# One decoder layer: output weights kept split for the second half, five banks for the gates, one PSUM pool

## The chip, the cores and the metric

The kernel runs on one core of a Trainium2 chip. The metric is the device time of one execution in microseconds. Before the change three runs took 2130.45, 2126.56 and 2125.76 us, with a median of 2126.56.

## The reference

One layer of a causal decoder, 1024 positions, 1024 features, all in float32. Two token mixers work side by side: a sparse attention (an indexer picks up to 256 keys for each query) and a stick-breaking attention. Their outputs are projected by `w_o_a` and `w_o_b`, gated, added, and projected by `w_out` into the residual stream. A gated feed-forward network stands before and behind.

```python
x = x + 1/2 * swiglu(rms_norm(x, g_ffn1), w1_gate, w1_up, w1_down)
proj = rms_norm(x, g_mix) @ w_in        # c_q, k_a, v_a, k_idx, w_idx, q_b, k_b, v_b, gate_a, gate_b
y_a = dsa_attention(...)                # (1024, 512), 8 heads of 64
y_b = stick_breaking_attention(...)     # (1024, 512)
merged = sigmoid(gate_a) * (y_a @ w_o_a) + sigmoid(gate_b) * (y_b @ w_o_b)
x = x + merged @ w_out
x = x + 1/2 * swiglu(rms_norm(x, g_ffn2), w2_gate, w2_up, w2_down)
```

## The kernel before

**Arithmetic.** TensorE multiplies in a rounded 32-bit format. To keep float32 accuracy every operand is held as a high part (rounded) and a low part (what the rounding left), and a product is three matmuls, high by high, high by low and low by high: `mm3`, lines 312 to 314. To split a weight, ACT copies it into the high part and POOL subtracts (`split`, lines 299 and 301; in the attention stage lines 1124 and 1126); `halve` does this for activations (lines 386 and 387). Weights that are needed twice can be kept in DRAM as parts: `split_of` names them, and line 1115 loads such parts without any splitting. In names, a last "h" or "l" is the part, and "r" is the raw weight.

**Stages.** The feed-forward network before runs to about 660 us, then come the projections of the mixers. From about 740 to 1368 us runs the stage "attend", in which both attentions, the gates' projections and the output projections of the first half of the positions are woven into one list. Then the second half of the positions is merged ("psm", to 1391 us: y of the sparse attention by `w_o_a`, times the gate on line 2262, plus the other mixer's part). Then `project` multiplies by `w_out`, for the first half to 1436 us and for the second to 1484 us ("psout"; the sum goes into x on line 2294), and the second feed-forward network runs to the end. Between the two projections' ends, x is normalised for that network: squares on ACT (line 428), mean and root (`rsqrt`, lines 288 and 290, the root on POOL), the product "by" on DVE (line 434), and transposes of "by" on TensorE ("pst", line 448).

**Order.** Each engine takes its own list strictly in order. Outside "attend" a scheduler writes the lists. Inside, the class `Weave` does: each piece of work is a generator that yields the engine of its next step and what it needs, and `Weave` gives every step a time from a cost estimate (`cost`) and always takes the one that can start first. The lists come from these estimates alone. All loads from DRAM stand in SP's list, most stores in POOL's (`put_low`).

**Buffers.** A `Ring` hands out a fixed number of buffers, and who wants one waits until it is given back. Accumulators in PSUM come from rings of banks: three "ubank", two "vbank", one "wbank", two "fbank". The gates' projections ("psf", in `fproj`) and the values' ("psuv", in `proj_uv`) use "fbank". A gate's bank is emptied by ACT's sigmoid into an "ev" buffer (`gate_out`, lines 1230 to 1235), of which there are three, and which comes free when POOL's store of it into `gd` has landed; "psuv" needs two of the three (`uv_out`, lines 1241 to 1248). The output weights "oa0", "oa2", "oa4", "oa6" (columns of `w_o_a` for the first half) and behind them "woa0" and "woa2" (the same weights again, for the second half) go through a ring of two raw buffers and one of four part buffers, that is two weights at a time.

**The attention's end.** A head's output leaves "pso" through ACT and DVE ("yt", lines 1891 and 1893) and is split into "y" (ACT line 2085, DVE line 2087). "psL" are the logits (lines 2037 and 2038), which DVE takes out of PSUM with their maximum "mx" (line 1991). "psoa" is the product of y by "oa". "y10" to "y13" are pairs of heads of the second half, y13 the last.

## Time and profile before

| | |
|---|---|
| three runs | 2125.76 to 2130.45 us, median 2126.56 |
| the profiled execution | 2126.26 us, span 2124.5 us |
| TensorE (PE) busy | 2100.6 us, 99% of the span, 10196 instructions |
| DVE, ACT, POOL busy | 1521.6, 1063.6 and 913.5 us (72, 50 and 43%) |
| DMA | 387.79 MB, 183 GB/s in the mean |
| 600 to 700 us | PE busy 97.85 of 100 us |
| 1040 to 1130 us | PE busy 86.99 of 90 us |
| 1300 to 1345 us | PE busy 42.44 of 45 us |
| 1460 to 1520 us | PE busy 59.39 of 60 us |

Times in the profile are microseconds from the start of the span. PE is TensorE, PEld its loading of weights, DVE VectorE, ACT ScalarE, POOL GpSimd, SP the engine whose queue issues the loads. A row of the timeline has the start, the duration, the engine, the line, the operation and "out<-in"; "x4" means that four instructions are drawn together; the bracket tells how long the engine had been idle and what released it. Ends of matmuls are modelled, so the distance between starts says more than their durations.

### The profile page before, as it was taken

How to read it: one execution, taken by the hardware profiler on the slowest of the kernel's cores; microseconds unless marked ns; L12 is line 12 of the kernel's file. 1: busy time of each engine (PE TensorE's matmuls, PEld its weight loads, DVE VectorE, ACT ScalarE, POOL GpSimd, SP SyncE). 2: the span in 40 equal slices, each digit the busy share in tenths (PEclk: the TensorE clock that was granted, in tenths of full speed). 3: DMA queues.
4: the chain of work that ended last, by engine and by line, in shares of the span. 5: the costliest groups of instructions: out<-in, count | busy, mean ns of one | idle time of the engine just before them, and what ended most of it. 6: DMA issues, size and time to landing. Idle time of an engine off the chain costs nothing.

```text
span 2124.5 us, 29820 instructions
## 1 busy us (share of the span) xinstructions
PE 2100.6 (99%) x10196; PEld 1762.4 (83%) x10196; DVE 1521.6 (72%) x2477; ACT 1063.6 (50%) x1998; POOL 913.5 (43%) x717
## 2 busy tenths in 40 slices
PE   8999999999999999999999999999999999999999
PEld 7888888888889988888887888778888888888887
DVE  7866767678875599788886588754755556488675
ACT  6343343334455356888886577535432322324443
POOL 6654555522345234322123342255665545542233
PEclk9999999999999999999999999999999999999999
DMA  5577877497685253686647755574143333259655
GB/s 150 160 245 219 251 203 237 151 328 249 212 231 167 76 159 105 224 217 165 171 157 231 258 165 169 190 257 151 50 129 100 104 95 129 95 185 330 222 175 188
DMA packets 298104, 387.79 MB, mean 183 GB/s; under 512 B 40144, under 2 KB 186224, under 8 KB 297952
## 3 DMA queue, kind: packets, MB, share of 16 engines
q1 hardware_dynamic: 285088, 343.90, 52.2%
q0 software_dynamic: 12864, 41.99, 5.5%
q8 instruction: 80, 1.31, 0.3%
q14 instruction: 72, 0.59, 0.1%
HBM read 264.67 MB, written 121.15 MB: 182 GB/s over the span
## 4 chain that ended last, share of the span: by engine, by line
PE 88%; issue 4%; DVE 3%; DMA 3%; POOL 1%; ACT 1%; SPq 0%; POOLq 0%; DVEq 0%; ACTq 0%
PE p L774 6%; PE p L775 6%; PE p L773 6%; PE pd L535 4%; PE pd L534 3%; PE pd L536 3%; PE pc L534 3%; PE pa L535 3%; PE pa L534 3%; PE pa L536 3%; PE pc L535 3%; PE pc L536 3%; PE psf L312 3%; PE psf L313 3%; PE psf L314 3%
## 5 line engine op out<-in xcount | busy, mean ns | idle before, releaser
L1374 ACT ACTIVATE junka<-u,cand,sig 128x1024 bf16<-128x1024 f32 (+3 forms) x124 | 134.5, 1085 | 5.0 <-DVE cand L1366 3.6
L1820 DVE TENSOR_TENSOR_SCAN left<-left,hidden 128x640 f32<-128x640 f32 (+3 forms) x64 | 88.9, 1409 | 2.0 <-ACT left L1814 1.8
L897 ACT ACTIVATE swh<-swr 128x512 fp32r<-128x512 f32 x48 | 30.2, 629 | 115.5 <-issue 52.5
L898 DVE TENSOR_TENSOR swr<-swr,swh 128x512 f32<-128x512 f32 x48 | 43.6, 908 | 37.8 <-ACT swh L897 37.6
L677 ACT ACTIVATE b0u<-b0u 128x512 f32<-128x512 f32 x20 | 12.6, 632 | 99.8 <-DVE b0u L557 84.4
L1874 DVE SCALAR_TENSOR_TENSOR pt<-pstT,pt 128x512 fp32r<-128x512 f32 (+1 forms) x96 | 51.4, 547 | 14.4 <-ACT pt L1871 13.8
L1871 ACT ACTIVATE pt<-pstT 128x512 fp32r<-128x512 f32 (+1 forms) x96 | 46.6, 495 | 16.6 <-PE pstT L1946 15.1
L1726 ACT ACTIVATE relu<-psdot 128x512 f32<-128x512 f32 (+1 forms) x80 | 40.7, 522 | 26.5 <-DVE u L1733 17.4
L1235 POOL DMA_DIRECT2D gd<-evg x32 | 18.0, 564 | 80.4 <-ACT evg L1230 59.4
L774 PE MATMUL p<-aT,aS 128*128 128x512 f32 x132 | 51.5, 390 | 1.0 <-DVE aT L387 1.0
L774 PE MATMUL p<-bT,bS 128*128 128x512 f32 x132 | 51.3, 389 | 0.0
L1733 DVE SCALAR_TENSOR_TENSOR u<-relu,WI,u 128x512 f32<-128x512 f32 (+1 forms) x70 | 49.2, 718 | 2.7 <-ACT relu L1726 1.7
L775 PE MATMUL p<-aT,aS 128*128 128x512 f32 x132 | 50.7, 389 | 0.0
L775 PE MATMUL p<-bT,bS 128*128 128x512 f32 x132 | 50.7, 389 | 0.0
L2000 ACT ACTIVATE e<-e,mx 128x768 f32<-128x768 f32 (+7 forms) x54 | 40.9, 759 | 13.3 <-DVE mx L1991 13.1
L773 PE MATMUL p<-bT,bS 128*128 128x512 f32 x132 | 47.0, 389 | 0.0
L1946 PE MATMUL pstT<-ident,left 128*128 128x128 f32 x288 | 45.8, 272 | 0.0
L773 PE MATMUL p<-aT,aS 128*128 128x512 f32 x132 | 44.9, 389 | 0.0
L1814 ACT ACTIVATE left<-psz 128x512 f32<-128x512 f32 (+2 forms) x96 | 43.4, 507 | 1.7 <-PE psz L1839 1.6
L1946 PEld LDWEIGHTS pstT<-ident,left 128*128 128x128 f32 x288 | 35.7, 140 | 8.2
L1370 DVE TENSOR_SCALAR_CACHE_REDUCE junkv<-u,cand 128x512 uint8<-128x512 f32 (+1 forms) x62 | 41.7, 673 | 0.8
L386 ACT ACTIVATE bT<-bt 128x512 fp32r<-128x512 f32 x44 | 26.2, 624 | 30.9 <-PE p L775 26.7
(3065 smaller groups left out, 8135.4 us busy)
## 6 DMA issues: line engine op xcount, KB each, us to landing
aw<-in_w_down_dram SPq DMA_DIRECT2D x33, 512.0 KB, 4.9
bw<-in_w_down_dram SPq DMA_DIRECT2D x33, 512.0 KB, 5.0
swr<-in_w_in_dram SPq DMA_DIRECT2D x48, 256.0 KB, 5.6
a0r<-in_w_gate_dram SPq DMA_DIRECT2D x22, 512.0 KB, 7.5
a1r<-in_w_up_dram SPq DMA_DIRECT2D x22, 512.0 KB, 7.2
b0r<-in_w_gate_dram SPq DMA_DIRECT2D x22, 512.0 KB, 4.1
b1r<-in_w_up_dram SPq DMA_DIRECT2D x22, 512.0 KB, 3.9
x<-in_x_dram SPq DMA_DIRECT2D x16, 512.0 KB, 6.2
```

What stands on the lines that cost most here:

```text
L312: nc.tensor.matmul(ps, ah, bh, start=first, stop=False)
L313: nc.tensor.matmul(ps, ah, bl, start=False, stop=False)
L314: nc.tensor.matmul(ps, al, bh, start=False, stop=last)
L534: nc.tensor.matmul(ps, a[:, c], b[k][:, HI], start=start and k == 0, stop=False, skip_group_check=True)
L535: nc.tensor.matmul(ps, a[:, c], b[k][:, LO], start=False, stop=False, skip_group_check=True)
L536: ins = nc.tensor.matmul(ps, a[:, l], b[k][:, HI], start=False, stop=k == 3, skip_group_check=True)
L773: nc.tensor.matmul(ps[q][m], S[:, h], T[:, HI], start=p == 0, stop=False)
L774: nc.tensor.matmul(ps[q][m], S[:, h], T[:, LO], start=False, stop=False)
L775: nc.tensor.matmul(ps[q][m], S[:, l], T[:, HI], start=False, stop=p == last)
L1374: nc.scalar.activation(junks[1][:, 0:(i + 1) * P], score[i], AF.Sign, scale=sig[:, b:b + 1], bias=cand.bitcast(F32)[:, b:b + 1], accum_out ...
L1820: nc.vector.tensor_tensor_scan(back, back, ones, 1.0, op0=ALU.mult, op1=ALU.max)
L1946: nc.tensor.transpose(tp[:, q * P:(q + 1) * P], A[n + q][:, j * P:(j + 1) * P], ident)
```

## The change

Six things change together; TensorE does the same matmuls.

1. *Parts kept.* While "oa" is used in "attend", a new stream `weights_out` stores its parts into DRAM as "woa0" to "woa6", and the merge of the second half loads them. In `project` the first half stores its parts of `w_out`, and the second half loads them. 12 raw loads with their 12 copies on ACT and 12 subtractions on POOL go, 24 stores on POOL's queue and 24 loads of parts on SP's come.
2. *Banks for the gates.* Between the marks "sparse" and "warm", gates and "psuv" may use "ubank" as well as "fbank" (`filling`), whichever is free first.
3. *Scattered durations.* `Weave` multiplies each estimated duration, except TensorE's, by a random factor between 0.97 and 1.03 (fixed seed).
4. *One PSUM pool.* One pool serves all stages, with the banks by name, where each stage had one of its own.
5. *The merge's order.* In "psm" the first four blocks take y10 to y12 first and y13 later, in an order that is written out.
6. *Steps.* POOL's subtraction of the "oa" weights goes in four steps of 256 columns.

The diff, cut to its core (in the changed kernel lines lie 4 to 59 lines further down):

```diff
@@ class Weave
+        self.luck = random.Random(67)
...
                 cost, late = self.cost(i, eng, outs, ins)
+                cost *= self.luck.uniform(1 - 0.03, 1 + 0.03) if eng != PE else 1.0
@@ def banks
+            turn[letter] += 1
+            return (first if letter == "a" else psum).tile([P, 512], F32, tag=f"{letter}{1 - turn[letter] % 2}", name=name, bufs=1)
@@ split_of: the parts that are kept in DRAM
+                for nm in (*columns, *(f"woa{d}" for d in range(0, ND, 2)), *(f"wout{n}{j}" for n in range(2) for j in range(0, ND, 2)))}
@@ PSUM pools
-    fpsum = ctxf.enter_context(tc.tile_pool(name="psf", bufs=1, space=PSUM))
+    fpsum, psum = (ctxf.enter_context(tc.tile_pool(name=f"ps{name}", bufs=1, space=PSUM)) for name in "fx")
...
-        ubank, vbank, wbank = (ring_of(tiles_of(psum), tag, bufs, (P, 512)) for tag, bufs in (("u", 3), ("v", 2), ("w", 1)))
-        fbank = ring_of(tiles_of(fpsum), "a", 2, (P, 512))
+        ubank, vbank, wbank = (bank_ring(psum, *tags) for tags in (("b0", "b1", "c0"), ("c1", "d0"), ("d1",)))
+        fbank = bank_ring(fpsum, "a0", "a1")
@@ def weights
-                nc.gpsimd.tensor_tensor(wl[:, 0:m], raw[:, 0:m], f32(wh[:, 0:m]), op=ALU.subtract)
+                step = 256 if nm[:2] == "oa" else m
+                for c in range(0, m, step):
+                    yield POOL, raw, wh
+                    c = slice(c, c + step)
+                    nc.gpsimd.tensor_tensor(wl[:, c], raw[:, c], f32(wh[:, c]), op=ALU.subtract)
@@ gates
+        def filling():
+
+            return [fbank, ubank] if "sparse" in weave.marks and "warm" not in weave.marks else [fbank]
+
+        def first_of(rings):
+            return min(rings, key=lambda r: weave.when((r,), PE))
...
-            ps = fbank("psf")
+            ps = first_of(rings or [fbank])("psf")
...
-            ps, vt, (uvh, uvl) = fbank("psuv"), VT[t], UV
+            ps, vt, (uvh, uvl) = first_of(rings)("psuv"), VT[t], UV
@@ attend's outputs
+        def weights_out(nm, *parts):
+            for to, w in zip(split_of[nm], parts):
+                weave.held[w.tensor.name] += 1
+                yield POOL, w
+                put_low(to, f32(w))
+                give(w)
...
+                if nm == "oa":
+                    spawn(weights_out(f"woa{d}", *W.parts))
@@ the merge of the second half
-                wh, wl = first.pop(0) if first else wcols(w_o_a, d * P, 2 * P, 0, 4, f"woa{d}")
...
-                    for k in range(4):
-                        c = slice((2 * k + e) * P, (2 * k + e + 1) * P)
-                        mm3(ps, wh[:, c], wl[:, c], Y[1][k][:, HI], Y[1][k][:, LO], k == 0, k == 3)
+            def output_weights(d):
+                if first:
+                    return first.pop(0)
+                W = [rpool.tile([P, 1024], F32R, tag="r", name=f"woa{d}{part}", bufs=NR) for part in "hl"]
+                for w, part in zip(W, split_of[f"woa{d}"]):
+                    nc.sync.dma_start(f32(w), part)
+                return W
...
+            with tc.manual_schedule(engines={nc.tensor.engine}):
+                at = {(d, e): begun(d, e, W[d], range(3)) for d, e in pairs[:4]}
+                for d, e in pairs[:4]:
+                    ended_(d, e, onward(d, e, W[d], (3,), at[d, e]))
+                for d, e in pairs[4:]:
+                    ended_(d, e, begun(d, e, W[d], range(4)))
@@ def project
-                        Ws[j] = wcols(w_out, n * 512, 512, j, 2, f"wout{half}{n}{j}", rawt=raw, wt=op)
+                        kept = split_of[f"wout{n}{j}"]
+                        if half:
+                            Ws[j] = [op(f"wout1{n}{j}{x}") for x in "hl"]
+                            for w, d in zip(Ws[j], kept):
+                                nc.sync.dma_start(f32(w), d)
+                        else:
+                            Ws[j] = wcols(w_out, n * 512, 512, j, 2, f"wout0{n}{j}", rawt=raw, wt=op)
+                            for w, d in zip(Ws[j], kept):
+                                nc.gpsimd.dma_start(d, f32(w))
```

Three places in TensorE's list, and one in SP's. First TensorE in the stage "attend", at the gate blocks wg1 and wg2, before:

```order
L1926 MATMUL psy_11206<-pt_11197,vv_10720 128x256 [waits Activation_49]
L1928 MATMUL psy_11206<-pt_11197,vv_10720 128x256 [waits DVE_49]
L1926 MATMUL psy_11206<-pt_11215,vv_10720 128x128 [waits Activation_49]
L1928 MATMUL psy_11206<-pt_11215,vv_10720 128x128 [waits DVE_49]
L312 MATMUL psf_11253<-mhi0_5617,wg1h_10898 128x512 [waits Activation_49]
L313 MATMUL psf_11253<-mlo0_5625,wg1h_10898 128x512
L314 MATMUL psf_11253<-mhi0_5617,wg1l_10899 128x512
```

The first matmul into the bank psf_11253 waits for ACT. So do, 24 rows on, the next two banks' first rows, for DVE and for ACT:

```order
L312 MATMUL psuv_11297<-uvh_8838,vt_11241 128x512 [waits DMAHW3_49,DVE_49]
L313 MATMUL psuv_11297<-uvl_8839,vt_11241 128x512
L314 MATMUL psuv_11297<-uvh_8838,vt_11241 128x512 [waits DMAHW4_49]
L312 MATMUL psf_11330<-mhi0_5617,wg2h_11125 128x512 [waits DMAHW7_49,Activation_49]
L313 MATMUL psf_11330<-mlo0_5625,wg2h_11125 128x512
```

After the change the same matmuls read:

```order
L316 MATMUL psf_11265<-mhi0_5641,wg1h_10955 128x512
L317 MATMUL psf_11265<-mlo0_5649,wg1h_10955 128x512
L318 MATMUL psf_11265<-mhi0_5641,wg1l_10956 128x512
L316 MATMUL psf_11265<-mhi1_5642,wg1h_10955 128x512
L317 MATMUL psf_11265<-mlo1_5650,wg1h_10955 128x512
```

There is no wait here, and at the next two banks:

```order
L316 MATMUL psuv_11324<-uvh_8889,vt_11176 128x512 [waits DMAHW1_49]
L317 MATMUL psuv_11324<-uvl_8890,vt_11176 128x512
L318 MATMUL psuv_11324<-uvh_8889,vt_11176 128x512 [waits DMAHW2_49]
L316 MATMUL psf_11335<-mhi0_5641,wg2h_11160 128x512 [waits DMAHW7_49]
L317 MATMUL psf_11335<-mlo0_5649,wg2h_11160 128x512
L318 MATMUL psf_11335<-mhi0_5641,wg2l_11161 128x512 [waits DMAHW0_49]
```

The matmuls are the same ones. The waits for ACT and DVE at the first matmul of a bank are gone; those for loads are left.

Second, TensorE at the end of "attend" and the start of the merge, before ("pso" is the last head, "psm" the merge on the parts of woa0):

```order
L2102 MATMUL pso_13955<-pt_14001,vh_13709 128x128 x2
L2102 MATMUL pso_13955<-morep0_12157,vh_13709 128x256 [waits Activation_49]
L2102 MATMUL pso_13955<-morep0_12157,vh_13709 128x256 [waits DVE_49]
L312 MATMUL psm_14049<-y10_12153,woa0h_13869 128x512 [waits DVE_49]
L313 MATMUL psm_14049<-y10_12153,woa0h_13869 128x512
L314 MATMUL psm_14049<-y10_12153,woa0l_13870 128x512
```

and after, from the last matmuls on "oa6" to the first on "woa2":

```order
L316 MATMUL psoa_14035<-y03_11361,oa6h_13850 128x512
L317 MATMUL psoa_14035<-y03_11361,oa6h_13850 128x512
L318 MATMUL psoa_14035<-y03_11361,oa6l_13851 128x512
L316 MATMUL psm_14104<-y12_12175,woa0h_13948 128x512
L317 MATMUL psm_14104<-y12_12175,woa0h_13948 128x512
L318 MATMUL psm_14104<-y12_12175,woa0l_13949 128x512
L316 MATMUL psm_14117<-y10_12173,woa2h_14058 128x512 [waits DMAHW4_49,PE_49]
L317 MATMUL psm_14117<-y10_12173,woa2h_14058 128x512
L318 MATMUL psm_14117<-y10_12173,woa2l_14059 128x512 [waits DMAHW5_49]
```

Before, the first "psm" on woa0 followed the last "pso" and waited for DVE. Now the last "pso" stands ahead of the 12 rows of this "psoa", 21 rows of "psm" on y10 to y12 follow them, and the first matmul on "woa2h" waits for a load, three rows behind the last on "oa6l".

SP's list after, around that load ("woa2hd" is the stored part in DRAM, "gd" the gates):

```order
L2290 DMA gate_14101<-gd_108 128x512 [waits DMAHW3_49]
L1124 DMA woa2h_14058<-woa2hd_174 128x1024 [waits DMAHW4_49,DMASW6_49,PE_49]
L1124 DMA woa2l_14059<-woa2ld_175 128x1024 [waits DMAHW5_49,DMASW7_49,PE_49]
L2291 DMA gate_14101<-obd_117 128x512 [waits DMAHW6_49]
L2290 DMA gate_14114<-gd_108 128x512 [waits DMAHW7_49]
```

The load of woa2h waits for TensorE (PE), since its buffer held oa6h.

Third, TensorE where the first half's projection by `w_out` ends and the second half's begins, before ("psg" is a transpose of the gains):

```order
L313 MATMUL psout_14373<-wout016l_14500,m07_14223 128x512
L314 MATMUL psout_14373<-wout016h_14498,m07_14223 128x512
L414 MATMUL psg_14551<-ident_71,bg_14549 128x8 [waits DMAHW2_49,DVE_49]
L312 MATMUL psout_14595<-wout100h_14601,m10_14412 128x512 [waits DMAHW4_49,DMAHW5_49,DMAHW3_49,DMAHW6_49,DMAHW1_49,DMAHW7_49,DMAHW0_49,Activation_49]
L313 MATMUL psout_14595<-wout100l_14603,m10_14412 128x512 [waits Pool_49]
L314 MATMUL psout_14595<-wout100h_14601,m10_14412 128x512
```

and after:

```order
L318 MATMUL psout_14412<-wout016h_14543,m07_14253 128x512
L453 MATMUL pst_14782<-ident_71,by00_14602 128x128 [waits DVE_49,Activation_49]
L453 MATMUL pst_14789<-ident_71,by00_14602 128x128
L453 MATMUL pst_14796<-ident_71,by00_14602 128x128
L453 MATMUL pst_14782<-ident_71,by01_14603 128x128 [waits DVE_49,Activation_49]
L453 MATMUL pst_14789<-ident_71,by01_14603 128x128
L453 MATMUL pst_14796<-ident_71,by01_14603 128x128
L453 MATMUL pst_14782<-ident_71,by02_14604 128x128 [waits DVE_49,Activation_49]
```

Rows of the same kind follow for by02 and by03, and then:

```order
L453 MATMUL pst_14796<-ident_71,by03_14605 128x128
L453 MATMUL pst_14803<-ident_71,by00_14602 128x128 [waits DVE_49]
L453 MATMUL pst_14803<-ident_71,by01_14603 128x128
L453 MATMUL pst_14803<-ident_71,by02_14604 128x128
L453 MATMUL pst_14803<-ident_71,by03_14605 128x128
L316 MATMUL psout_14642<-wout100h_14646,m10_14455 128x512 [waits DMAHW7_49,DMAHW2_49,DMAHW1_49]
```

Before, the second projection followed at once. Now the 16 transposes of by00 to by03 stand between the two, each first one waiting for DVE and ACT, and the first matmul on "wout100h" is behind the last of them.

More of the change, by code (lines that the diff above doesn't have):

```diff
@@ L330, in in_turn, with banks @@
         return tile_
-    def banks(psum, first=None):
-        at = [0]
+    def banks(psum, first):
+        at, turn = [0], defaultdict(int)
         def bank(name, letter=None):
@@ L1062, in trunk @@
     fp = tc.tile_pool(name="sf", bufs=1)
-    psm = tc.tile_pool(name="psm", bufs=1, space=PSUM)
-    with fp as fpool, psm as psum, tc.manual_schedule(
+    with fp as fpool, tc.manual_schedule(
             engines={nc.tensor.engine, nc.vector.engine, nc.scalar.engine, nc.gpsimd.engine}):
@@ L1307, in fillers @@
                 for half in range(2):
-                    yield PE, fbank, late(3)
-                    ps, cols = yield from fproj(s.parts, half, lambda: late(3))
+                    rings = filling()
+                    yield PE, rings, late(3)
+                    ps, cols = yield from fproj(s.parts, half, lambda: late(3), rings)
                     outs.append(spawn(gate_out(ps, g, cols)))
@@ L1313, in fillers @@
                     t = len(UVS)
-                    if gates.index(g) >= UV_FROM and t < NT and weave.when(("uv", f"vt{t}", fbank), PE) <= weave.free[PE]:
+                    if gates.index(g) >= UV_FROM and t < NT and weave.when(("uv", f"vt{t}", filling()), PE) <= weave.free[PE]:
                         yield from proj_uv(t)
@@ L2241, in trunk @@
         heads_.close()
[L2244 removed]
+    with ctxf, tc.tile_pool(name="ring2", bufs=1) as rpool:
         op, raw = ring(rpool)
@@ new lines, in begun, with onward @@
+            def begun(d, e, W, ks):
+                r = slice((d + e) * P, (d + e + 1) * P)
+                g = ht("gate", F32)
+                nc.sync.dma_start(g[:, 0:512], gd[r, 512:1024])
+                nc.sync.dma_start(g[:, 512:1024], obd[r, 512:1024])
+                return onward(d, e, W, ks, (bank("psm", "bcda"[(d + e) % 4]), g))
+            def onward(d, e, W, ks, at):
+                for k in ks:
+                    c = slice((2 * k + e) * P, (2 * k + e + 1) * P)
+                    mm3(at[0], W[0][:, c], W[1][:, c], Y[1][k][:, HI], Y[1][k][:, LO], k == 0, k == 3)
+                return at
```

35 lines of the change are left out of this document (17 added, 18 removed).

## The prediction

> **What bounds the kernel now.** I read the busy times and the table of stretches first, then the waits of TensorE, then its timeline around each wait, and last the engines that end these waits. From the page and the table (columns: stretch in us, its length, busy us and instructions of PE, PEld, DVE, ACT, POOL, granted clock, DMA share, GB/s):
>
> ```profile
> PE 2100.6 (99%) x10196; PEld 1762.4 (83%) x10196; DVE 1521.6 (72%) x2477; ACT 1063.6 (50%) x1998; POOL 913.5 (43%) x717
> ...
> 1300.00:1345.00 45.00, 42.44 (x224) 34.45 (x223) 42.52 (x88) 31.87 (x57) 12.31 (x10) 1.00 0.58 182
> 1345.00:1400.00 55.00, 52.18 (x249) 42.56 (x249) 42.63 (x60) 25.36 (x39) 22.59 (x13) 0.97 0.55 192
> 1400.00:1460.00 60.00, 60.00 (x272) 49.58 (x271) 24.45 (x36) 23.31 (x32) 31.44 (x17) 1.00 0.75 261
> ```
>
> TensorE is busy 2100.6 of 2124.5 us, so the whole idle time that any edit can win is 23.9 us, while its instructions are as many after the change as before. Between 1400 and 1460 us it never stops: 272 matmuls in 60 us, one every 0.22 us, and this is why the splittings of weights that ACT and POOL no longer do win nothing there. A change shows only where TensorE waits, or where it stands in a new place behind something late. The waits of TensorE (line, releaser; total us, times, longest):
>
> ```profile
> PE psL L2037 <- DVE mx L1991: 2.4, 2, 2.2
> ...
> PE psdot L1755 <- ACT relu L1726: 1.7, 4, 0.6
> PE psf L312 <- ACT evg L1230: 1.5, 2, 1.2
> PE psf L312 <- DVE evl L1243: 1.5, 1, 1.5
> PE psm L312 <- DVE yt L1893: 1.4, 1, 1.4
> ...
> PE psout L313 <- POOL wout000l L301: 1.3, 1, 1.3
> ```
>
> The change comes to all of these but "psdot". I take them in order of time, and then two places where the new order makes TensorE wait.
>
> **Gates, more banks.** TensorE around the three waits of the gate projections (start, us, instruction; idle before it in brackets), then ACT's evictions and the landing of the stores from "evg":
>
> ```profile
> 1113.82 0.28 PE L1928 MATMUL psy<-pt,vv 128*128 128x128 f32 x1
> 1115.26 0.50 PE L312 MATMUL psf<-mhi,wg1h 128*128 128x512 f32 x1 [1.17 <-ACT evg L1230]
> ...
> 1121.29 0.39 PE L314 MATMUL psuv<-uvh,vt 128*128 128x512 f32 x1
> 1122.04 0.50 PE L312 MATMUL psf<-mhi,wg2h 128*128 128x512 f32 x1 [0.37 <-ACT evg L1230]
> ...
> 1127.39 0.39 PE L314 MATMUL psf<-mhi,wg2l 128*128 128x512 f32 x1
> 1129.25 0.50 PE L312 MATMUL psf<-mhi,wg2h 128*128 128x512 f32 x1 [1.47 <-DVE evl L1243]
> ```
>
> ```profile
> 1114.64 0.57 ACT L1230 ACTIVATE evg<-psf 128x512 f32<-128x512 f32 x1
> 1121.42 0.57 ACT L1230 ACTIVATE evg<-psf 128x512 f32<-128x512 f32 x1
> 1129.20 0.60 ACT L1230 ACTIVATE evg<-psf 128x512 f32<-128x512 f32 x1 [1.05 <-DMA gd<-evg]
> ```
>
> ```profile
> DMA to landing us min/median/max: 2.3/4.6/8.9
> ```
>
> From start to start, less 0.1 us for a matmul of 128 columns and 0.23 us for one of 512, the three cost 1.34, 0.52 and 1.63 us, 3.5 in all. The banks are held because their eviction waits for one of the three "ev" buffers, and these come free when a store has landed (median 4.6 us). In the new order none of these three rows waits for ACT or DVE, since five banks serve instead of two. The buffers are not more, though, so part may come back some banks later: bounds −3.5 and 0. ACT's evictions come 6.8 and 7.8 us apart, and one gate half with its "psuv" is 27 matmuls, 6.1 us: the lag is 0.7 to 1.7 us a round, and three banks more hold several rounds. I take −3.0.
>
> **Subtractions of w_o_a in four steps.** TensorE, DVE and POOL at the longest wait of all:
>
> ```profile
> 1340.15 0.39 PE L314 MATMUL psoa<-y,oa4l 128*128 128x512 f32 x1
> 1342.75 0.45 PE L2037 MATMUL psL<-kkh,qs 128*128 128x384 f32 x1 [2.21 <-DVE mx L1991]
> ```
>
> ```profile
> 1339.20 2.90 DVE L2087 TENSOR_TENSOR y<-yt,y 128x512 fp32r<-128x512 f32 x1
> ...
> 1342.62 0.68 DVE L2191 TENSOR_TENSOR o<-psoa,both 128x512 f32<-128x512 f32 x1
> ```
>
> ```profile
> 1339.18 2.38 POOL L1126 TENSOR_TENSOR oa6l<-oa6r,oa6h 128x1024 fp32r<-128x1024 f32 x1 [5.83 <-ACT oa6h L1124]
> ```
>
> DVE's subtraction of 128x512 takes 2.90 us where the like of it takes 0.68: it began 0.02 us after POOL's and ended after it. The 2.2 us that it was late are TensorE's 2.21. A step of 256 columns is an estimated 0.6 us (a quarter of 2.38), so DVE loses 0 to 0.6 us instead of 2.2. DVE is busy 42.5 of these 45 us, and gets a few divisions from ACT; at 0.7 us each (as the 0.68 of the row), one or two of them may land here. I take −1.9, bounds −2.2 and −0.5.
>
> **The last head.** TensorE where the second half's merge begins:
>
> ```profile
> 1367.07 0.85 PE L2102 MATMUL pso<-morep,vh 128*128 128x256 f32 x2
> 1369.32 0.53 PE L312 MATMUL psm<-y,woa0h 128*128 128x512 f32 x1 [1.41 <-DVE yt L1893]
> 1369.66 0.62 PE L313 MATMUL psm<-y,woa0h 128*128 128x512 f32 x1
> 1370.08 0.63 PE L314 MATMUL psm<-y,woa0l 128*128 128x512 f32 x1
> ...
> 1373.06 0.40 PE L312 MATMUL psm<-y,woa0h 128*128 128x512 f32 x1
> ```
>
> The wait is 1.41 us, and behind it the matmuls start 0.43 us apart until 1373.06 (the granted clock of the stretch is 0.97): eight steps in 3.40 us that take 1.8 at 0.23, so 1.6 more. With 0.45 us lost inside the pair at 1367.07 (0.85 where two of 256 columns need 0.4 at most), the place costs 3.5. In the new order 12 matmuls of "psoa" and 21 of "psm" stand between the last "pso" and the first that needs y13. They cover 33 x 0.23 = 7.6 us, and evicting the head took 2.25 us (1367.07 to 1369.32). All 3.5 go; bounds −3.5 and −1.9 (a slow stretch left to what comes).
>
> **Stored w_o_a, loaded late.** This is the first new wait. "woa2h" and "woa2l" get the buffers of "oa6h" and "oa6l". Their loads therefore stand in SP's queue until TensorE has finished the last "psoa", and in the new order only three matmuls (0.7 us) lie between that and the first one on "woa2h". In before, ACT and POOL split woa2 at 1359 us, so nothing waited. Of how long such a load of 512 KB takes the trace has the loads of the stored halves of other weights (L1115):
>
> ```profile
> L1115 SPq DMA_DIRECT2D wqk5200h<-wqk5200hd x1: 320/320/320, 679.5 to 679.5; - x1
> ...
> DMA to landing us min/median/max: 3.2/4.8/10.1
> ```
>
> At the least it costs 3.2 − 0.7 = 2.5 us, at the median 4.8 − 0.7 = 4.1; I take 3.8, nearer to the median, as queues are 0.55 busy here. Behind "woa2h" waits all the rest of TensorE's list; SP holds gate loads behind it that are needed later. The Trainium skill, "DMA: Bandwidth & Descriptors", section on the anatomy of one DMA, has about 2.0 us fixed and the bytes at 436 GB/s; by it, an estimate, 512 KB take 3.2 us. That is the least that the trace has, its median is 1.6 us over it, and the sum would be 1.3 us lower. The loads of woa0, woa4 and woa6 have some 28 matmuls or more ahead of their first use, 6.3 us and more, and I cost them nothing; if woa0's took the longest landing, it would be late by 10.1 − 6.3 = 3.8.
>
> **The border of the two projections.** The second new wait. TensorE and then DVE in before:
>
> ```profile
> 1436.07 0.39 PE L314 MATMUL psout<-wout016h,m 128*128 128x512 f32 x1
> 1436.54 0.50 PE L312 MATMUL psout<-wout100h,m 128*128 128x512 f32 x1
> ...
> 1458.48 3.65 PE L448 MATMUL pst<-ident,by 128*128 128x128 f32 x32
> ```
>
> ```profile
> 1436.49 0.69 DVE L2294 TENSOR_TENSOR x<-x,psout 128x512 f32<-128x512 f32 x1 [0.67 <-PE psout L314]
> ...
> 1437.67 0.15 DVE L288 TENSOR_SCALAR ms<-ss 128x1 f32<-128x1 f32 x1 [0.42 <-ACT by L428]
> ...
> 1441.67 0.14 DVE L288 TENSOR_SCALAR ms<-ss 128x1 f32<-128x1 f32 x1
> 1442.49 0.88 DVE L434 TENSOR_SCALAR by<-x,rs 128x512 f32<-128x512 f32 x2 [0.68 <-POOL rs L290]
> 1443.29 0.14 DVE L288 TENSOR_SCALAR ms<-ss 128x1 f32<-128x1 f32 x1
> ```
>
> The transposes of "by" run at 1458.48, 22 us after the last matmul of the first projection, long after "by" is ready. In the new order 16 of them stand directly behind that matmul and ahead of the first "wout100". They need the whole chain: the last addition into x starts 0.42 us after that matmul and takes 0.69; then per row tile a mean on DVE, a root on POOL and two products on DVE, 1.62 us (1441.67 to 1443.29), one tile after the other, as DVE's list has them. From 0.42 + 0.69 = 1.1 us, three tiles (4.9) and the fourth's first product (0.15 + 0.68 + 0.44 = 1.3) make 7.3; the second product and a copy of the gains (0.6) stand ahead of the last four transposes (0.11 each): TensorE goes on at about 8.4. In before it went on at 0.47. The 16 transposes are done meanwhile, 16 x 0.114 = 1.8. So 8.4 − 0.5 − 1.8 = 6.1; 6.6 if the first mean waits for ACT until 1.6 as in before, 4.5 if the chain starts early; I take 6.2. Behind so sparse a stretch I count one slow run like that at 1369, +1.6. That the loads of wout1 need no splitting changes nothing: they are asked for well ahead.
>
> **The rest.** "wout000l" is still split on POOL behind the last use of woa0; I count its 1.3 us unchanged. One PSUM pool costs nothing but order. The scattered durations reorder the list of the stage from 740 to 1368 us, in which, beside the places above, the 1.7 us of "psdot" are what can still go, and a wait like one of them what can come: 0, bounds −1.7 and +2.
>
> **The sum.** −3.0 − 1.9 − 3.5 + 3.8 + 6.2 + 1.6 = +3.2. The profiled execution took 2126.26 us (span 2124.5, 1.76 around it), 0.3 under the median of 2126.56: 2126.3 + 3.2 = 2129.5.
>
> **The rivals.** What a measurement of this kernel can tell from no change is about 0.2%, 4.25 us: under 2122.3 is faster, over 2130.8 slower.
>
> *The removed waits win.* They are worth −8.4, so this is the case wherever the two new waits stay under 4.4 us together. With the load at its least (2.5), the chain at its shortest without a slow stretch (4.5) and "psdot" gone too (−1.7), it is still 2123.6; with both hidden altogether, 2117.9. Against it: TensorE takes its list in order, and the chain's steps are measured. For it: the loads' least, 3.2, is measured too, and a new order of the list may give them more cover than I count. Chance 0.25.
>
> *The buffers take the banks' gain back.* This is the slow side. With five banks TensorE runs ahead, but three "ev" buffers and a landing of 4.6 us still set the drain; if the lag of 0.7 to 1.7 us a round outlasts three more banks, the waits come back in the gates that follow: +3.0, 2132.5. It decides if more than about three rounds of gate and "psuv" follow one another. For it: ACT's last eviction waited 1.05 us for a store's landing. Against: without "psuv" a gate half needs one buffer in 5.5 us. Chance 0.15.
>
> *The clock.* Between 1369 and 1373 us the clock fell after 1.41 us; after 2.21 us at 1342.75 it did not. If it falls behind the wait for woa2 as well, that is +1.6, 2131.1. The Trainium skill, "TensorE: Matmul & The Clock Gate", Part 1, has half speed after an idle window of some 3.4 us that runs free, and full speed after a busy one; it speaks against this change, both new waits being that long, while the trace's 1.41 us are less than it asks. Chance 0.12, half of it over 2130.8.
>
> *One of the two new waits is not there* (a load that starts earlier, a chain that overlaps): 2129.5 − 3.8 = 2125.7 or 2129.5 − 7.8 = 2121.7. Chance 0.1, half of it faster.
>
> **How the numbers follow.** My forecast has 0.38, its own range 2125 to 2133; of it 0.26 is within 0.2% and 0.12 over. Faster: 0.25 + 0.05 = 0.30. Slower: 0.12 + 0.15 + 0.06 = 0.33. Same: 0.26 + 0.06 + 0.05 = 0.37. The range, 2118 to 2136, reaches to both new waits hidden and to buffers and clock together (2134.1) with the list's 2.
>
> **What would show it.** Right: no wait of "psf" for ACT near 1115 to 1130; no wait over 1 us of "psL" for DVE with a DVE row of 2.9 under a POOL row; "psm" on woa2 idle 2.5 to 4.1 us behind a DMA; "pst" on "by" waiting for DVE, in pieces that add to about 6 us, ahead of "wout100", and 0.43 us steps behind. Wrong: "woa2h" landed before its row, transposes in one piece, or new waits over 3 us between 740 and 1300.

## The result and the profile after

The changed kernel takes 2153.97 us (median of four runs, 2151.86 to 2156.49), the kernel before 2127.17 us beside it: 1.0124 times as long, 95% interval 1.0107 to 1.0142, or 26.8 us more. The forecast was 2129.5 with a range of 2118 to 2136. The profiled execution of the changed kernel took 2153.77 us, span 2152.0, which is 27.5 us over the span before.

The busy times and the table of stretches of the changed kernel (columns as in the prediction):

```profile
PE 2111.7 (98%) x10196; PEld 1771.3 (82%) x10196; DVE 1513.5 (70%) x2481; ACT 1048.2 (49%) x1982; POOL 896.1 (42%) x741
```

```profile
0.00:70.00 70.00, 64.18 (x308) 53.84 (x309) 56.70 (x92) 43.51 (x75) 41.30 (x36) 0.98 0.49 139
700.00:750.00 50.00, 48.10 (x367) 47.11 (x368) 26.37 (x42) 17.30 (x40) 15.03 (x15) 0.97 0.17 62
1040.00:1130.00 90.00, 88.56 (x482) 74.79 (x481) 77.15 (x160) 79.39 (x168) 17.57 (x22) 1.00 0.51 152
...
1300.00:1345.00 45.00, 45.00 (x252) 38.32 (x251) 40.50 (x92) 31.70 (x59) 16.77 (x22) 1.00 0.63 216
1345.00:1400.00 55.00, 48.45 (x233) 38.85 (x232) 33.06 (x57) 18.83 (x33) 12.37 (x17) 0.97 0.85 306
1400.00:1460.00 60.00, 49.96 (x209) 39.36 (x207) 33.16 (x39) 17.65 (x27) 26.45 (x25) 0.92 0.90 330
```

TensorE has the same 10196 matmuls. The stretch from 1400 to 1460 us, which it filled with 272 matmuls before, now holds 209, with a granted clock of 0.92 and the DMA engines busy 0.90 of the time instead of 0.75. The two stretches in which the change was to remove waits did improve: 88.56 of 90 us busy at the gates (86.99 before), 45.00 of 45 near 1340 (42.44). What it costs lies elsewhere, and part of it in the first 70 us and around 700, which the prediction never looked at.

TensorE's waits between 1365 and 1470 us in the changed kernel (line, releaser; total us, times, longest):

```profile
PE pst L453 <- DVE by L439: 4.3, 3, 2.7
PE psout L316 <- ACT wout014h L303: 3.0, 1, 3.0
PE psm L316 <- DMA woa2h<-woa2hd: 2.8, 1, 2.8
PE psout L316 <- DVE gate L2303: 1.7, 1, 1.7
PE psout L317 <- POOL wout014l L305: 1.6, 1, 1.6
```

"woa2" and "by" are the two new waits of the prediction. "wout014" is in none of its terms.

**Where the 27 us are.** Waits alone don't tell it, since matmuls also run slowly behind them. So I took the distance from each matmul's start to the next one's and subtracted the normal one of its size (0.227 us for 512 columns, 0.109 for a transpose). What is left is lost time of TensorE, here by stretch for the two kernels and four of the experiments below, in us:

| stretch | before | after | pool alone (e10) | stores alone (e7) | four parts (e5) | three parts (e4) |
|---|---|---|---|---|---|---|
| 0 to 70 | 7.1 | 11.2 | 11.2 | 7.0 | 7.5 | 7.4 |
| 70 to 665 | 1.3 | 0.7 | 0.8 | 1.2 | 1.2 | 1.0 |
| 665 to 740 | 1.5 | 6.1 | 7.2 | 1.2 | 2.0 | 1.3 |
| 740 to 1080 | 8.3 | 11.0 | 8.1 | 8.4 | 12.2 | 8.3 |
| 1080 to 1200 | 5.8 | 3.2 | 5.8 | 6.0 | 1.6 | 1.3 |
| 1200 to 1300 | 2.2 | 2.2 | 2.1 | 2.3 | 2.3 | 12.8 |
| 1300 to 1366 | 5.6 | 2.9 | 5.5 | 5.5 | 1.9 | 1.5 |
| 1366 to 1400 | 5.9 | 8.8 | 1.8 | 4.2 | 3.6 | 3.6 |
| 1400 to 1520 | 1.4 | 16.3 | 9.9 | 12.5 | 1.5 | 1.4 |
| 1520 to the end | -0.1 | 3.9 | 3.0 | 0.0 | -0.1 | 0.0 |
| all | 39.0 | 66.1 | 55.4 | 48.4 | 33.6 | 38.6 |

The sums differ as the spans do: after less before is 27.1 (spans 27.5), e10 16.4 (16.4), e7 9.4 (9.5), e5 -5.4 (-5.1). A wait is booked where it ends.

### The profile page after: what moved, and what is told of

It reads as the page before. It is cut to its first block, busy times and chain, and to the rows that moved or that the text cites. A ratio compares the mean times of both kernels' runs of the same rounds, so it can differ in the third digit from the quotient of the medians.

```text
span 2152.0 us, 29884 instructions
## 1 busy us (share of the span) xinstructions
PE 2111.7 (98%) x10196; PEld 1771.3 (82%) x10196; DVE 1513.5 (70%) x2481; ACT 1048.2 (49%) x1982; POOL 896.1 (42%) x741
## 4 chain that ended last, share of the span: by engine, by line
PE 86%; DVE 5%; DMA 4%; issue 2%; ACT 2%; POOL 0%; SPq 0%; ACTq 0%; DVEq 0%; POOLq 0%
PE p L779 6%; PE p L780 6%; PE p L778 6%; PE pa L539 4%; PE pa L541 4%; PE pa L540 4%; PE pc L539 3%; PE pd L539 3%; PE pd L541 3%; PE pc L541 3%; PE pc L540 3%; PE pd L540 3%; PE psf L316 3%; PE psf L318 3%; PE psf L317 3%
## 5 line engine op out<-in xcount | busy, mean ns | idle before, releaser
L1395 ACT ACTIVATE junka<-u,cand,sig 128x896 bf16<-128x896 f32 (+3 forms) x124 | 134.2, 1082 | 3.4 <-DVE cand L1387 1.8
L904 DVE TENSOR_TENSOR swr<-swr,swh 128x512 f32<-128x512 f32 x48 | 43.5, 906 | 33.6 <-ACT swh L903 33.4
L1747 ACT ACTIVATE relu<-psdot 128x512 f32<-128x512 f32 (+1 forms) x80 | 39.9, 522 | 29.4 <-DVE u L1754 20.1
```

The source lines that it names most:

```text
L1395: nc.scalar.activation(junks[1][:, 0:(i + 1) * P], score[i], AF.Sign, scale=sig[:, b:b + 1], bias=cand.bitcast(F32)[:, b:b + 1], accum_out ...
```

## The experiments

The theory at the start was that the new order of PSUM banks and the traffic of the stores make the loss, and the planned gains are there; the rivals were that the scattered list is what costs, or the two predicted waits alone. There are twelve kernels, e1 to e12. They were timed in three groups, and differences in us are to the median of the kernel before in the same group (2128.01, 2128.96, 2127.99).

### Taking parts out of the changed kernel

**The banks.** The PSUM pools, and with them the choice of banks, are those of before.

```diff
-            turn[letter] += 1
-            return (first if letter == "a" else psum).tile([P, 512], F32, tag=f"{letter}{1 - turn[letter] % 2}", name=name, bufs=1)
+            return (first if letter == "a" else psum).tile([P, 512], F32, tag=letter, name=name, bufs=2)
...
-        ubank, vbank, wbank = (bank_ring(psum, *tags) for tags in (("b0", "b1", "c0"), ("c1", "d0"), ("d1",)))
+        ubank, vbank, wbank = (ring_of(tiles_of(psum), tag, bufs, (P, 512)) for tag, bufs in (("u", 3), ("v", 2), ("w", 1)))
```

> The changed kernel with the PSUM pools of before (a pool for each stage, two buffers to a tag) and all else as changed. Theory 'banks by turn': the fixed turn of bank names is what makes TensorE wait at the start of both feed-forward networks (+4.1 and +3.9 us against before) and reorders the projections at 660 to 740 us (+4.7); those 12.7 us go, the weights' 17.7 us stay: about 2141. Rival 'stored parts are all of it' (the DMA traffic and the late loads make the whole loss, the network's waits come with another order anyway): within 3 us of 2154.

2141.97 us, ratio 1.0066 (1.0051 to 1.0081). That is 14.0 over before, so the one pool is 12.8 of the 26.8, and the other half stays without it. The waits of that half are not all the same ones: here TensorE waits 5.2 us for a "gate" in the merge and 5.9 us for the load of the gains ("bg") at the border.

**The stores.** No part of w_o_a or w_out is stored; the second half loads raw weights and splits them, as before (the merge of the second half too, not shown).

```diff
-                for nm in (*columns, *(f"woa{d}" for d in range(0, ND, 2)), *(f"wout{n}{j}" for n in range(2) for j in range(0, ND, 2)))}
+                for nm in (*columns,)}
...
-                if nm == "oa":
-                    spawn(weights_out(f"woa{d}", *W.parts))
...
+                        Ws[j] = wcols(w_out, n * 512, 512, j, 2, f"wout{half}{n}{j}", rawt=raw, wt=op)
```

> The changed kernel without any stored parts: w_o_a and w_out are loaded raw and split again for the second half, as before; all else as changed. Theory 'stored parts': between 1366 and 1520 us the changed kernel loses 25 us to waits and slow steps where before lost 7.3, and 3.5 of these 7.3 are gone by the new order of the merge; so 17 to 21 us go: 2133 to 2137. Rival 'one pool': the waits between 1366 and 1520 come from banks taken by turn, and less than 6 us go: 2148 or more.

2136.05 us, 1.0036 (1.0023 to 1.0048): +8.0, so the stores and what hangs on them cost 18.8. Without them TensorE loses 0.3 us between 1400 and 1460 instead of 13.5: the wait for wout014 and the pieces of the border go together, and the transposes of "by" stand behind wout106 again, as in before.

**w_out alone.** Parts of w_o_a are stored, those of w_out are not.

```diff
-                for nm in (*columns, *(f"woa{d}" for d in range(0, ND, 2)), *(f"wout{n}{j}" for n in range(2) for j in range(0, ND, 2)))}
+                for nm in (*columns, *(f"woa{d}" for d in range(0, ND, 2)))}
...
+                        Ws[j] = wcols(w_out, n * 512, 512, j, 2, f"wout{half}{n}{j}", rawt=raw, wt=op)
```

> The changed kernel without the stored parts of w_out alone; the parts of w_o_a are stored and loaded as changed. Theory 'stored parts': the wait for wout014 with its slow steps (7.5 us) and the transposes at the border of the two projections (5 to 7 us) go, the wait for woa2 (5 us with its slow steps) stays: about 2140, 4 to 6 us over the kernel without any stored parts. Rival 'w_o_a is the main part': at most 5 us go, 2149 or more.

2141.6 us, 1.0065 (1.005 to 1.008). So of the 18.8 the parts of w_out are 13.2 (26.8 - 13.6) and those of w_o_a 5.6 (13.6 - 8.0). The 5.6 look like the predicted wait for woa2, 3.8 and 1.6 for the clock, but the traces don't bear that out. This kernel waits 2.9 us for the load of woa2h; the one without any stores, which splits the raw weights, waits there as well:

```profile
PE psm L318 <- POOL woa2l L1138: 2.0, 1, 2.0
PE psm L318 <- POOL woa4l L305: 1.8, 1, 1.8
PE psm L316 <- ACT woa2h L1133: 1.0, 1, 1.0
```

By the measure of the table it loses 9.0 us between 1366 and 1400, and this one 10.3: 1.3 more. The profiled spans of the two are 2.8 us apart. What the rest of the 5.6 is stays open.

### Where the bank order costs

**The pool alone.** The kernel before, with the one pool and its turns as the only change (the edit is that of the first experiment, turned round).

> The kernel before with one PSUM pool and banks by turn, and nothing else. Theory 'banks by turn': the first block of either feed-forward network loses 3.8 to 4.1 us, and the projections at 660 to 740 us 4 to 5: 2138 to 2141. Rival 'only together with the other parts': within 3 us of before.

2143.27 us, 1.0066 (1.005 to 1.0083): +15.3, more than I expected. Its longest waits of TensorE:

```profile
PE psout L312 <- ACT wout000h L299: 3.6, 1, 3.6
PE pscqt L1550 <- DMA cqn<-cqd: 2.5, 1, 2.5
...
PE psout L313 <- POOL wout000l L301: 2.1, 1, 2.1
PE pa L535 <- DVE asg L664: 1.9, 1, 1.9
PE pa L535 <- DVE bsg L664: 1.9, 1, 1.9
```

In before "pscqt" waited 1.20 us and "wout000l" 1.3; the other three were not there. The wait for "wout000h" is not there in the changed kernel either: of the 16.4 us in the table, 4.4 are the balance from 1366 to 1520, where this kernel loses otherwise than the changed one. How a name for a bank makes a wait is best seen at "pa", in the first feed-forward network of the changed kernel. TensorE and then DVE (start, us; the bracket is the idle time before):

```profile
57.76 0.39 PE L541 MATMUL pd<-aB,a10S 128*128 128x512 f32 x1
60.10 0.47 PE L539 MATMUL pa<-aB,a01A 128*128 128x512 f32 x1 [1.95 <-DVE asg L668]
...
61.80 0.63 PE L539 MATMUL pa<-aB,a01A 128*128 128x512 f32 x1
62.22 0.63 PE L540 MATMUL pa<-aB,a01A 128*128 128x512 f32 x1
...
64.75 0.40 PE L540 MATMUL pc<-aT,a10A 128*128 128x512 f32 x1
```

```profile
56.87 2.48 DVE L500 TENSOR_TENSOR aT<-ar,aT 128x512 fp32r<-128x512 f32 x4
59.28 0.67 DVE L668 TENSOR_TENSOR asg<-asg,pa 128x512 f32<-128x512 f32 x1
```

In before this "pa" began at 53.74 us, woven between the matmuls of "pc", and waited for nothing. With strict turns it gets the bank whose old content DVE takes out only at 59.28, behind four subtractions. TensorE stops for 1.95 us and then starts matmuls 0.43 us apart: from 57.76 to 64.75 us 14 steps take 6.99 us where 3.18 is normal, 3.8 lost. The same happens in the second network at 1552.70 us. Around 700 us, with the matmuls of the projections in another order, "cq" is loaded late: the load is issued 6.6 us after that of before (698.08 and 691.51), of which some 4 were lost earlier, and "pscqt" waits 2.92 us in the changed kernel.

**One turn taken back.** In the changed kernel one block's transposes take a bank of letter "a" without moving its turn on.

```diff
+            still, letter = letter == "A", letter.lower()
             turn[letter] += 1
+            if still:
+                turn[letter] -= 1
+                return first.tile([P, 512], F32, tag=f"a{turn['a'] % 2}", name=name, bufs=1)
...
-            R.turn("B12", "cdab", (r["T1"], r["T3"]))
+            R.turn("B12", "cdAb", (r["T1"], r["T3"]))
```

> The changed kernel, but the transposes of B12 in the feed-forward network's first block take the bank of name a that is next without moving the turn on, so that the accumulator after them does not get the bank of the one that DVE reads late. Theory 'banks by turn': the waits of pa for DVE at 60 and 1552 us (2.1 us each) and the slow steps behind them go, 7 to 8 us: 2146. Rival 'one pool costs by something else than the turn': 2152 or more.

2149.09 us, 1.0098 (1.0083 to 1.0113), 6.7 less than the change itself (20.1 over before instead of 26.8). Both waits of "pa" are gone, and the loss in the first 70 us is 7.3 instead of 11.2, which shows the mechanism. But the same edit lengthened the wait of "pscqt" to 4.1 us and that for "wout014h" to 4.2.

### The stores by themselves

**Stores that nobody reads.** The kernel before, with the first half's parts of w_out stored; the second half still loads raw weights.

```diff
+                        if not half:
+                            for w, d in zip(Ws[j], split_of[f"wout{n}{j}"]):
+                                nc.gpsimd.dma_start(d, f32(w))
```

> The kernel before, and the parts of w_out are stored into DRAM during the first projection, but nobody loads them: the second half splits them again. So 8 MB more are written and the loads are as before. Theory 'traffic': the loads of wout014 and after come late by the stores, and TensorE waits for them: 4 to 8 us more than before, 2131 to 2135. Rival 'order': the stores are hidden, and what cost in the changed kernel is where loads and transposes stand in the lists: within 2 us of before.

2142.12 us, 1.0061 (1.004 to 1.0081). More than I expected, and with the same loads. TensorE in this kernel, where the last weights of the first half come in:

```profile
1427.83 1.20 PE L312 MATMUL psout<-wout014h,m 128*128 128x512 f32 x4 [2.49 <-ACT wout014h L299]
1430.36 0.80 PE L313 MATMUL psout<-wout014l,m 128*128 128x512 f32 x1 [1.33 <-POOL wout014l L301]
```

This is the wait of the changed kernel. The stretch from 1400 to 1440 us, first in before and then here (columns as above), and the time from issue to landing of one load of 512 KB in it, in before and here:

```profile
1400.00:1440.00 40.00, 40.00 (x177) 32.83 (x176) 14.80 (x21) 15.96 (x21) 20.40 (x10) 1.00 0.83 295
```

```profile
1400.00:1440.00 40.00, 35.22 (x147) 28.09 (x146) 11.54 (x17) 10.31 (x14) 19.68 (x18) 0.96 1.00 371
```

```profile
m14r<-md SPq DMA_DIRECT2D x1, 512.0 KB, 10.0
...
wout014r<-in_w_out_dram SPq DMA_DIRECT2D x1, 512.0 KB, 4.1
```

```profile
m14r<-md SPq DMA_DIRECT2D x1, 512.0 KB, 17.6
```

The DMA engines were already busy 0.83 of this stretch. Sixteen stores of 512 KB, 8 MB, twelve of them issued in it, fill it to 1.00 at 371 GB/s, and the load of merged rows "m14r" takes 17.6 us instead of 10.0. The raw load of wout014 itself lands in 4.2 us, as in before. It is issued late, at 1422.41 us instead of 1415.40, each time 0.84 us after ACT has split "m10", which landed after 14.3 us instead of 7.5.

This is one half of it: 5.8 us are lost at wout014, from 1424 to 1436. Another 4.6 are lost from 1442 to 1455, since the stores also changed the list that the scheduler wrote: 16 transposes of "by", which before has at 1458 behind wout106, now stand among the first matmuls on wout100 and wait for DVE. So the kernel doesn't separate the traffic from the order.

**The same stores, small.** As above, with 64 of the 1024 columns stored.

```diff
-                                nc.gpsimd.dma_start(d, f32(w))
+                                nc.gpsimd.dma_start(d[:, 0:64], f32(w)[:, 0:64])
```

> As the run with stores that nobody loads (2142, profiled 2136), with the same 16 stores on POOL's queue, but of 64 of the 1024 columns: a sixteenth of the bytes. Theory 'traffic': the loads of the merged rows land as in before (7.5 to 10 us, where the full stores made it 14 to 18), wout014 is asked for in time, and nothing is lost: within 2 us of before. Rival 'POOL's queue': the issuing of stores between the subtractions holds these up, and 5 us or more stay.

2131.17 us, 1.0014 (1.0004 to 1.0024): 3.2 us are left of 13.2. The number of stores and their issues on POOL's queue are the same, so about 10 us hang on the bytes. They do so in two ways, since with the small stores the transposes stand behind wout106 again, and the losses at both places are down to some 1 us each. POOL's queue explains at most the 3.2 us. How the 10 us divide between the DMA engines and the scheduler's list is read from the trace (5.8 and 4.6) and not from a run.

### The planned gains

**Three parts.** Banks for the gates, steps and late heads only: no pool, no stores, no scattered durations. Pools and weights are taken back as in the first two experiments, and besides:

```diff
-                cost *= self.luck.uniform(1 - 0.03, 1 + 0.03) if eng != PE else 1.0
```

> Only three of the six parts: five banks for the gates, subtractions of w_o_a in four steps, the merge's first blocks with the last heads late. Pools and weights as before, durations not scattered. Theory 'the waits named do go': the prediction's own terms, -3.0, -1.9 and -3.5, without the new waits: 2118, with bounds 2116 and 2122. Rival 'the new list of the attention stage costs as much as the banks win' (the changed kernel loses 3.1 us more than before at 740 to 850 us): 2121 to 2125.

2127.16 us, 0.9998 (0.9989 to 1.0007). This was my clearest miss: the three terms of the prediction were worth 8.4, and nothing shows. By the table they are there: 4.5 us less lost at 1080 to 1200, 4.1 less at 1300 to 1366, 2.3 less at 1366 to 1400, 10.9 in all. But 10.6 are lost anew at 1200 to 1300, where before lost 2.2:

```profile
1209.47 1.31 PE L2145 MATMUL pspT<-ident,e 128*128 128x128 f32 x10 [2.75 <-DVE e L2032]
...
1238.21 0.80 PE L2122 MATMUL pso<-pt,vh 128*128 128x512 f32 x1 [1.27 <-DVE pt L1897]
```

These steps of the attention wait for DVE. One reason could be that the gates, which fill TensorE between such steps, are finished too soon: their last bank is emptied at 1201.6 us, at 1205.0 in before. But the whole program is 4.5 us ahead of before at 1200 us by the table, and with another seed (below) the last bank is emptied at 1212.9 us and 9.4 us are lost all the same. Why this list waits here is open.

**Two parts.** As before it, but gates keep their two banks.

```diff
-            return [fbank, ubank] if "sparse" in weave.marks and "warm" not in weave.marks else [fbank]
+            return [fbank]
```

> Only two of the six parts: subtractions of w_o_a in four steps, and the merge's first blocks with the last heads late. Theory 'the banks win their 3.7 us at 1080 to 1130 and give back 10 at 1200 to 1250': without them the list stays as in before up to 1300 us, and the two parts win 3.9 (1300 to 1345) and 2.2 (1366 to 1400): 2120 to 2121. Rival 'the steps or the merge shift the waits at 1200 to 1250': 2126 or more.

2124.79 us, 0.9982 (0.9973 to 0.9991). Steps and late heads give 4.2 us, of the 6.1 that I expected. The banks, in this list, take 3.3 of it away (0.9 are left in the run of three parts).

**Four parts.** The three, and the scattered durations with the change's seed, 67.

```diff
+                cost *= self.luck.uniform(1 - 0.03, 1 + 0.03) if eng != PE else 1.0
```

> As the run with three of the six parts (2127), and the planner's durations scattered as in the change. In the run with three parts TensorE lost 11.4 us between 1200 and 1250 us where before lost 1.1 and the changed kernel 1.2, and 2.1 us between 800 and 850 us where the changed kernel lost 5.8. Theory 'the scattered list moves both places': about 10 us less at the one, 4 to 6 us more at the other: 2121 to 2123. Rival 'the 11 us belong to the five banks and stay, whatever the list': 2130 to 2133.

2121.26 us, 0.9966 (0.9956 to 0.9977): faster than both kernels, by 7.7 us than before. The stretch from 1200 to 1300 loses 2.3 again, nearly as little as in before (2.2). In return "psdot" waits for ACT in four places, 4.0 us (1.7 before), in the stretch from 740 to 1080.

**Another seed.** Four parts, seed 68.

```diff
-        self.luck = random.Random(67)
+        self.luck = random.Random(68)
```

> The four parts that won, with another seed of the scatter (68 in place of 67). Theory 'the scatter is a draw of lots': the waits of the attention stage fall in other places and sum to something between the list without scatter (2127) and 2117; no preference for 2121, a difference of 3 us or more from it either way. Rival 'any scatter spreads the waits': 2119 to 2123 again.

2134.15 us, 1.0027 (1.0017 to 1.0036), outside what even the theory of a draw allowed; the rival, that any scatter helps, falls. Here 9.4 us are lost from 1200 to 1250.

**Scatter in the second part only.** Four parts, with the durations scattered only once the mark "sparse" is reached.

```diff
-                cost *= self.luck.uniform(1 - 0.03, 1 + 0.03) if eng != PE else 1.0
+                cost *= self.luck.uniform(1 - 0.03, 1 + 0.03) if eng != PE and "sparse" in self.marks else 1.0
```

> The four parts that won (2121.3: five banks, steps, late heads, scattered durations), with the scatter only from the mark sparse on, so that the list up to 850 us is that of before. Theory 'the scatter loses at 800 to 850 and wins at 1200 to 1250': the 4.9 us more that the four parts lost at 800 to 850 go, and the later places stay: 2116 to 2117. Rival 'another draw, another list': the draws fall on other steps, and the 10 us at 1200 to 1250 come back in part: 2121 to 2128.

2129.11 us, 1.0006 (0.9997 to 1.0016). My hope was to keep the gain and lose the waits of "psdot". They are back at 1.7 us and the loss from 740 to 850 at 4.4, as in before, but 13.6 us are lost from 1200 to 1250. Same parts, four lists: 2127.2, 2121.3, 2134.2 and 2129.1 us.

**The sum.** Four parts -7.7, the pool +15.3 and the stores +18.8 make +26.4; the change measured +26.8. The first two come from kernels that hold no part of the others (e5, e10), and -7.7 + 15.3 = 7.6 stands against 8.0 for both together (e2). That it comes out so well is luck in part. By stretches the losses don't add up: from 1366 to 1400 us e5 loses 3.6, e10 1.8 and e2 9.0, and from 1400 to 1520 e10 loses 9.9 and e2 1.4.

## Why the prediction was wrong

Most of its terms for the places it looked at held in size; it failed on the steps that it priced at nothing: the one PSUM pool, the stores, and the new list. In its own order:

**Gates** (-3.0): the three waits are gone, and 1080 to 1200 loses 2.6 us less (5.8 to 3.2). That the gain stays was not shown by this: in the list of three parts it is lost again 100 us later. The rival of the "ev" buffers did not come; a wait of "psy" for ACT did, 1.44 us at 1124.88.

**Subtractions in steps** (-1.9): 1300 to 1366 loses 2.7 less. DVE's splitting of y, POOL's steps on oa6 and a DVE addition beside them, in the changed kernel:

```profile
1344.61 0.68 DVE L2108 TENSOR_TENSOR y<-yt,y 128x512 fp32r<-128x512 f32 x1
```

```profile
1350.57 3.29 POOL L1138 TENSOR_TENSOR oa6l<-oa6r,oa6h 128x256 fp32r<-128x256 f32 x4 [0.17 <-ACT oa6h L1133]
```

```profile
1352.14 1.12 DVE L2215 TENSOR_TENSOR o<-o,both 128x512 f32<-128x512 f32 x1
```

The split of y took 0.68 us where it had taken 2.90, but it no longer stands beside POOL: the steps come 6 us behind it. The addition that does stand beside them takes 1.12 us, 0.43 more than its median of 0.69, which is within the 0 to 0.6 of the prediction. So the size is right, and that a step holds DVE up for less fits; whether the 2.7 us come from the steps or from the new place in the list, no run here separates.

**The last head** (-3.5): the wait and the slow run are gone. Right.

**woa2** (+3.8, and the clock as a rival at +1.6). TensorE and SP:

```profile
1374.73 0.39 PE L318 MATMUL psm<-y,woa0l 128*128 128x512 f32 x1
1377.96 0.47 PE L316 MATMUL psm<-y,woa2h 128*128 128x512 f32 x1 [2.84 <-DMA woa2h<-woa2hd]
...
1379.21 0.80 PE L318 MATMUL psm<-y,woa2l 128*128 128x512 f32 x1 [0.54 <-DMA woa2l<-woa2ld]
...
1382.31 0.39 PE L316 MATMUL psm<-y,woa2h 128*128 128x512 f32 x1
```

```profile
1374.24 0.32 SPq L1124 DMA_DIRECT2D woa2h<-woa2hd  x1
```

The load is issued at 1374.24, when the last "oa6" is read, and lands 3.6 us later; TensorE goes on at 1377.96. From 1374.73 to 1382.31 ten steps take 7.58 us, 2.27 would be normal: 5.3 lost, 3.7 in waits and 1.6 in slow steps. Mechanism and size were right, and the clock rival came as well. The kernel without the stores (e2) loses nearly as much in this stretch, by other waits.

**The border** (+6.2 and +1.6). TensorE:

```profile
1452.13 0.39 PE L318 MATMUL psout<-wout016h,m 128*128 128x512 f32 x1
1455.22 0.52 PE L453 MATMUL pst<-ident,by 128*128 128x128 f32 x3 [2.70 <-DVE by L439]
1456.85 0.52 PE L453 MATMUL pst<-ident,by 128*128 128x128 f32 x3 [1.11 <-ACT by L433]
1458.46 0.87 PE L453 MATMUL pst<-ident,by 128*128 128x128 f32 x3 [1.09 <-DVE by L439]
...
1461.44 2.05 PE L316 MATMUL psout<-wout100h,m 128*128 128x512 f32 x4
```

The transposes wait in pieces, 1.6 us apart, as the chain of the prediction has them. TensorE goes on 9.3 us after the last matmul (forecast 8.4): 9.3 - 0.5 - 1.8 = 7.0, and 1.4 in slow steps behind it.

With what was measured for them these terms make up -2.6 - 2.7 - 3.5 + 5.3 + 8.4 = +4.9. The rest of the 26.8, some 22 us, is in three sentences of the prediction that gave a reason for nothing, or none. By the table it lies at 0 to 70, 665 to 740 and behind 1520 us (4.1, 4.6 and 4.0: the pool), at wout014 (7.3: the stores) and at 740 to 1080 (2.7: the list).

*"One PSUM pool costs nothing but order."* The order is the cost: 13 us (12.8 when it is taken out of the changed kernel, 12.7 by the rows just named). At "pa" it was readable before the run, since in the new list of TensorE this matmul waits for DVE and had no such wait in the old one. I compared the order at the places the change names, and not at those it merely passes through.

*"That the loads of wout1 need no splitting changes nothing: they are asked for well ahead."* True for the loads; the stores that feed them were given no price. In the changed kernel the last raw weights of the first half come too late. TensorE, SP and ACT:

```profile
1433.89 0.39 PE L318 MATMUL psout<-wout012h,m 128*128 128x512 f32 x1
1437.32 0.79 PE L316 MATMUL psout<-wout014h,m 128*128 128x512 f32 x1 [3.04 <-ACT wout014h L303]
1439.75 0.79 PE L317 MATMUL psout<-wout014l,m 128*128 128x512 f32 x1 [1.64 <-POOL wout014l L305]
...
1443.73 0.39 PE L317 MATMUL psout<-wout014l,m 128*128 128x512 f32 x1
```

```profile
1423.82 1.37 SPq L301 DMA_DIRECT2D wout014r<-in_w_out_dram  x1
```

```profile
1436.21 1.06 ACT L303 ACTIVATE wout014h<-wout014r 128x1024 fp32r<-128x1024 f32 x1 [0.41 <-DMA wout014r<-in_w_out_dram]
```

The raw load was issued 8.4 us later than in before (1415.40), which is no more than the program was behind at 1400 us by the table (8.4). But it landed some 12 us later, where it took 4.1. ACT and POOL split it only then, and TensorE loses 7.3 us: 9.84 for eleven steps that need 2.50. The profile of before had the DMA share of this stretch, 0.75, in a quoted row; I read from it that TensorE never stopped, and not that a quarter of the DMA engines' time was all that 8 MB of stores could use. The border's term, too, hangs on them: without the parts of w_out, or with small stores, the transposes stay where before has them.

*"The scattered durations reorder the list ...: 0, bounds -1.7 and +2."* The bounds were too narrow by several times: 6 us better than none with one seed, 7 worse with the next. In the changed kernel the stretch from 740 to 1080 us loses 2.7 more, of which 2.4 are "psdot" (4.1 after 1.7); the new waits between 740 and 1300 us come to over 3 us, one of the prediction's signs of being wrong.

Smaller: that "wout000l" stays unchanged was wrong, since its 1.3 us are gone and a wait for "gate" (1.7) stands there; "woa0" costs 0.7. The first rival's lowest sum is 2126.3 - 8.4 + 2.5 + 4.5 - 1.7 = 2123.2, not 2123.6. And the idle 23.9 us were not all that could be won, since by the measure above before loses 39.0 with its slow steps.

Open: why the bank turns alone make "wout000" late at 1400 us in e10 (the load was issued at 1393.19 us and took 7.0 us to land; no run tests a part of this by itself); what the 5.6 us of the parts of w_o_a are; why the seeds place their waits where they do; and why stores alone cost 13.2 us in the timed runs and 9.5 in the profiled one.

## What to carry to other kernels

Price the bytes of a store that saves work, at the DMA share of the stretch it runs in: with the queues at 0.75 to 0.83, 8 MB of writes cost more than the eight splittings and raw loads of w_out they replaced, which were hidden. And look at the lists again, since a scheduler may move other work for them. A rule that names banks by turn can put a matmul behind a late reader that it never met before; compare the waits of the whole order, also in stages that the change doesn't mean to touch. And where a planner sets the order, a gain at one wait is a gain only after the next 100 us have been read, and one draw of its durations says little about another: four lists of the same work spread over 13 us.

## What the hardware showed that I had not expected

One DVE subtraction beside POOL took 8.19 us, twelve times the 0.69 of the next one like it. DVE and POOL in the changed kernel:

```profile
1403.13 8.19 DVE L392 TENSOR_TENSOR m<-gate,m 128x512 fp32r<-128x512 f32 x1 [1.02 <-ACT m L391]
```

```profile
1402.47 2.41 POOL L305 TENSOR_TENSOR wout002l<-wout002r,wout002h 128x1024 fp32r<-128x1024 f32 x1
...
1405.41 2.40 POOL L305 TENSOR_TENSOR wout004l<-wout004r,wout004h 128x1024 fp32r<-128x1024 f32 x1
...
1408.35 2.41 POOL L305 TENSOR_TENSOR wout006l<-wout006r,wout006h 128x1024 fp32r<-128x1024 f32 x1
```

The next one like it is at 1412.62. The slow one did not get in between POOL's three subtractions, although POOL issued a store for about 0.6 us between each two and ended after the last. The Trainium skill, "SBUF — State Buffer", section on the two separate sides, has a lock on the ports that the two engines share, held for one instruction, with the other engine fully blocked. The trace agrees that DVE is blocked; that it lost three times in a row is not stated there.

Slow steps followed short waits here too, as after the 1.41 us that the prediction read at 1369: after 1.95 us at 60.10 the steps turn to 0.43 us some 1.3 us later and stay so for 3.0 us, with a granted clock of 0.50 from 61.4 to 64.3. The Trainium skill, "TensorE: Matmul & The Clock Gate", Part 1, asks for an idle window of some 3.4 us; no wait of TensorE in this place is that long, so the trace doesn't bear this out as a lower limit.
